# One output product per FFN over all middle values, with every transpose of those values through the DMA crossbar, in a float32 decoder trunk

## The chip, the cores and the metric

The kernel runs on one core of a Trainium2 chip. The metric is the device time of one execution in microseconds. The core has five engines that run at once and are tied together by semaphores: TensorE (PE in the profile, with PEld for its weight loads), VectorE (DVE), ScalarE (ACT), GpSimd (POOL) and SyncE (SP). SP issues plain DMAs, POOL issues DMAs that add into their target. Each engine runs its instructions in the order of the program.

## The reference

Two layers over 512 positions of width 1024, all in float32. Layer 0 mixes positions with a gated linear recurrence, layer 1 with a spatial gating unit; each mixer stands between two half-weighted feed-forward networks (FFNs) with 2816 middle values:

```python
def swiglu(x, w_in, w_out):
    g, u = jnp.split(x @ w_in, 2, axis=-1)
    return (jax.nn.silu(g) * u) @ w_out

for i in range(DEPTH):
    h = h + 0.5 * swiglu(rms_norm(h, ffn1_norm[i]), ffn1_w_in[i], ffn1_w_out[i])
    m = recurrent_mixer(...) if i % 2 == 0 else spatial_gating_mixer(...)   # on rms_norm(h, mix_norm[i])
    h = h + m
    h = h + 0.5 * swiglu(rms_norm(h, ffn2_norm[i]), ffn2_w_in[i], ffn2_w_out[i])
return rms_norm(h, final_norm)
```

So there are four FFNs. The change touches the first three: FFN 1 (before the recurrence), FFN 2 (after it) and FFN 3 (before the spatial mixer).

## The kernel before

**A product in float32.** Each float32 operand is split into a high part that TensorE's fp32r format holds and the low rest (`Sub.split`, `split`): ACT copies the high part (L97), DVE subtracts it (L88). A product is then three matmuls: high by high, low by high, high by low (L415 to L417).

**Seven products for eight.** A product of two matrices is cut into 2 x 2 blocks and made with seven block products, P1, P2, P5, P6, P3, P7, Q4, by the Winograd scheme (`seven`, L368). The left block of each is A11, A12, S1, S2, S4, S3, A22 (`LEFT`), where S1 = A21 - A22, S2 = S1 - A11, S4 = S2 + A12, S3 = -S2 - A22 are made by DVE (`Group.s2`, `s4`, `s3`). The right blocks are sums of weight blocks. A tile of raw weights (128 x 1024 floats, 512 KB) is loaded by SP (L136), and other blocks are added into it, either by an accumulating DMA from POOL (L139; `plus` is one soon after the load, `then` one after the tile's split) or by DVE from a second tile. Eight raw tiles can be live (`RAW_BUFS`, `load_more`).

**Steps.** The program is one list of steps, `subs`. A step is one of the seven products over one pair of 128-wide tiles of the contracted side: two row tiles, two tiles of the pair, three matmuls, 12 in all. The loop at L1623 walks the list: at step i it splits the weights of the steps up to i + 3 (`SPLIT_AHEAD`), runs the hooks planned for this step (phases pre, mid, rest), starts loads, and then issues the matmuls. When the last pair of a product is done, its post reads the PSUM banks. PSUM banks are named in `BANK`: P1, P6, P7 accumulate on A, P2 has B, P5 and P3 share C; Q4 has A in a chunk and its own bank Q in an output product.

**An FFN.** The 22 tiles of middle values are made in parts (`FF_PARTS`): a plain pair and a chunk of four, then twice two chunks of four. A chunk (`chunk`, L798) is one set of seven products, 14 steps, for the gate and the other half together, with SiLU and the multiplication in its posts; P3's post finishes the rows of the upper half, Q4's those of the lower. A pair (`pair_plain`, L846) is made without the scheme. Each part is followed at once by its output product (`out_blocks`, L632), seven products over the part's pairs, whose posts add 16 times into x (`upd`, L650).

**Transposes.** The middle values come out with positions on the partitions; the output product needs them the other way. Each group (one chunk or pair) is turned block by block in one of two ways (`left_blocks`, L744). By PE (`Group.stage`, `turn`, L264): transposes against an identity into PSUM (L268), from where ACT copies three blocks and DVE makes S1 of the fourth. Or by the DMA crossbar (`Group.cross`, L298), which moves 16-bit halves: ACT copies the two 16-bit planes apart (`pl`), SP issues the crossbar transposes (`dt`, L314), and five and six steps later ACT merges the planes again. In each part the pair or the first chunk of a two-chunk part goes through the crossbar, the other chunk through PE.

**Norms.** The output product of the last part calls the next norm (`norm.quarter`) as each quarter of x is done: after P2, P3, P7 and Q4.

Of the kernel before, what the change touches and what calls it, by code (L numbers as in the profile page):

```python
# [12 lines left out]
ALU = mybir.AluOpType  # L13

P = 128
# [13 lines left out]


FF_PARTS = (("p", 4), (4, 4), (4, 4))

RAW_BUFS = 8
SPLIT_AHEAD = 3
# [19 lines left out]
def trunk(ctx: ExitStack, tc: tile.TileContext, a: dict, out: bass.AP):  # L54
# [32 lines left out]
    def tt(o, x, y, op):  # L87
        nc.vector.tensor_tensor(out=o, in0=x, in1=y, op=op)  # L88
# [127 lines left out]
    def hook(n, phase, fn):  # L216


        hooks.setdefault((n, phase), []).append(fn)
# [29 lines left out]
    class Group:  # L249


        def __init__(self, n):
            self.n, self.f, self.hl = n, {}, {}
# [112 lines left out]
        return left  # L366

    def seven(block, cuts, left, w, posts, order=None, own=False, apart=False, joined=None, opening=None,  # L368
              also=None):

# [9 lines left out]
        bk, raw, held = {}, {}, []  # L380
# [49 lines left out]
        for prod, ci in order:  # L430
            if opening and (prod, ci) == ("P5", 0):
                opening[2]()

            def new(k, n, plus=None, wait=2):
                b = lambda k, n: block(k, n, cuts[ci])
                return raw_of(b(k, n), [P, len(cuts[ci]), w], plus and b(*plus), wait)

            tile = then = tile_then = None
            if prod == "P1":
                r = raw[11, ci] = new(0, 0)  # L440
                if again(ci):
                    then = block(0, 1, cuts[ci])
            elif prod == "P2":
                r = new(1, 0)
            elif prod == "P5":
                if again(ci):
                    pass
                elif own:
                    raw[11, ci] = new(0, 0, (0, 1))
                    if far(ci):  # L450
                        then = block(1, 1, cuts[ci])
                else:
                    tile = raw[12, ci] = new(0, 1)
                    tile_then = block(1, 1, cuts[ci])
                r = raw[11, ci]
            elif prod == "P6" and joined:

                tile, r, then = new(0, 1, (1, 1)), new(0, 0), block(1, 0, cuts[ci])
                raw[6, ci], raw[12, ci] = r, tile
            elif prod == "P6" and far(ci):  # L460
                r, then = raw[11, ci], block(1, 0, cuts[ci])
            elif prod == "P6":
                r, tile, then = raw[11, ci], new(1, 1), block(1, 0, cuts[ci])
                raw[22, ci] = tile
            elif prod == "P3":
                r = new(1, 1) if far(ci) or joined else raw[22, ci]
            elif prod == "P7":
                r = raw[12, ci] if joined or not own else new(0, 1, (1, 1), 2 + ci if far(ci) else 2)
            else:
                r = raw[6 if joined else 11, ci]  # L470
            subs.append(Sub(r, mm_of(prod, ci), None, tile, then, tile_then))
# [157 lines left out]
                hook(n + 4, "pre", lambda: self.take(1))  # L629


    def out_blocks(w, k0, groups, scale, norm=None, order=None, own=False, soon={}, swap=False, p2_lag=0):  # L632

        n = [g for g in groups]
        cuts, bases, i, r = [], {}, 0, k0
# [82 lines left out]
        if ends:  # L718
            order = norm.ORDER
        order = seven(block, cuts, left_of(lambda: [gs[i] for i in range(len(n))]), 512,  # L720
                      dict(P1=p1, P2=p2, P5=p5, P6=p6, P3=p3, P7=p7, Q4=q4), order, own, not ends,
                      "P3" if ends else None, also=norm.gather if ends else None)
# [75 lines left out]
    def chunk(w_in, f0, nt, group, opening=None, whole=False):  # L798


        w = nt * P
        c1, c2, c3, c5, ht = {}, {}, {}, {}, {}

        def rt(t):
            return S.rt[:, t : t + 1]

        def new(d, s, name):
            d[s] = slot(name=name)[:, :w]
            return d[s]

        def p1(s, ps):
            act(new(c1, s, "c1"), ps, AF.Copy)

        def p2(s, ps):
            tt(c1[s], c1[s], ps, ALU.add)
            hook(now[0] + (9 if opening else 1), "mid", lambda: act(c1[s], c1[s], AF.Silu, scale=rt(s)))

        def p5(s, ps):
            act(new(c5, s, "c5"), ps, AF.Copy)

        def p6(s, ps):
# [87 lines left out]

    def ffn(w_in, w_out, norm):  # L910
        f0 = 0
        for i, sizes in enumerate(FF_PARTS):
            groups, p0, pair, first = [], f0, None, not subs
            for j, n in enumerate(sizes):
                if n == "p":
                    groups.append(Group(1))
                    pair = lambda g=groups[-1], f0=f0: pair_plain(w_in, f0, g, first)
                    if not first:
                        pair()
                    f0 += 2  # L920
                else:
                    groups.append(Group(n // 2))
                    chunk(w_in, f0, n, groups[-1], (opening["A11"], opening["A12"], pair) if first else None, j == 0)
# [4 lines left out]
            soon = {("Q4", 1): 3} if last and isinstance(norm, TileNorm) else {}  # L928
# [737 lines left out]
```

## Time and profile before

| | |
|---|---|
| median of 3 runs | 1596.77 us (1595.55 to 1597.46) |
| the profiled execution: time, span | 1596.2 us, 1594.5 us |
| mean granted TensorE clock | 0.998 |
| busy PE, DVE, ACT, POOL | 1584.9, 1370.3, 1099.0, 222.2 us |
| moved by DMA | 289.79 MB, 182 GB/s on average |

The span is from the first to the last instruction. Busy time is the time in which an engine has an instruction in work; matmuls overlap each other, so that of PE says that it is occupied, not at what rate. In a group's row stand line, engine, operation, target and sources, shape and count, then busy time and mean duration in nanoseconds, then the idle time of the engine before these instructions and what ended it. In a row on a stretch stands, for each engine, its busy time in it with the number of its instructions, then granted clock, the DMA engines' mean busy share and GB/s. A wait's row gives who waited for whom, in total, how often, and the longest.

### The profile page before, as it was taken

What the parts mean: (1) busy time and instruction counts of PE and PEld (TensorE: products, weight loads), DVE (VectorE), ACT (ScalarE), POOL (GpSimd) and SP (SyncE); (2) the same over time, 40 slices, a digit from 0 to 9 for tenths busy, and PEclk for the clock granted to TensorE, in tenths of its full rate; (3) what the DMA queues carried; (4) which work ended last, traced back from release to release, by engine and by line L of the source; (5) the groups of instructions that cost most, each with busy time, mean ns of one, the idle gap of its engine ahead of it and who ended that gap; (6) DMA issues with size and microseconds to landing.
All of it is one profiled execution on the core that took longest, in us unless ns stands there. A gap on an engine that the chain in (4) does not pass through costs nothing.

```text
span 1594.5 us, 20905 instructions
## 1 busy us (share of the span) xinstructions
PE 1584.9 (99%) x7293; PEld 1313.9 (82%) x7293; DVE 1370.3 (86%) x1846; ACT 1099.0 (69%) x1615; POOL 222.2 (14%) x201
## 2 busy tenths in 40 slices
PE   9999999999999999999999999999999999999998
PEld 7878888898888888888888888888888888888886
DVE  6998887888998888978988978878978989889788
ACT  7757658668777657557776575586886876675676
POOL 2111111100010211111101111111211011111120
PEclk9999999999999999999999999999999999999999
DMA  8868878843384788878838798788878567796793
GB/s 288 193 168 194 208 177 197 209 139 106 92 211 100 178 202 207 202 175 193 201 104 195 169 201 208 181 192 203 219 197 201 158 132 198 179 223 167 175 233 94
DMA packets 208296, 289.79 MB, mean 182 GB/s; under 512 B 55504, under 2 KB 81216, under 8 KB 208192
## 3 DMA queue, kind: packets, MB, share of 16 engines
q1 hardware_dynamic: 158688, 195.33, 39.9%
q0 software_dynamic: 47712, 91.30, 34.0%
q10 hardware_dynamic: 1792, 1.84, 0.4%
q8 instruction: 57, 0.93, 0.2%
q14 instruction: 47, 0.39, 0.1%
HBM read 275.84 MB, written 2.10 MB: 174 GB/s over the span
## 4 chain that ended last, share of the span: by engine, by line
PE 94%; DMA 3%; DVE 1%; issue 0%; ACT 0%; SPq 0%; POOL 0%; POOLq 0%; ACTq 0%; DVEq 0%
PE A L415 14%; PE A L416 14%; PE A L417 14%; PE C L416 8%; PE C L417 8%; PE C L415 8%; PE p L864 4%; PE B L416 4%; PE B L417 4%; PE B L415 4%; PE e L268 2%; DMA raw<-in_ffn_w_in_dram 2%; PE r L226 2%; PE r L228 2%; PE r L227 2%; PE Q L415 1%
## 5 line engine op out<-in xcount | busy, mean ns | idle before, releaser
L97 ACT ACTIVATE whi<-raw 128x1024 fp32r<-128x1024 f32 (+1 forms) x537 | 554.7, 1034 | 330.8 <-PE A L416 78.3
L88 DVE TENSOR_TENSOR wlo<-raw,whi 128x1024 fp32r<-128x1024 f32 (+1 forms) x537 | 637.2, 1189 | 167.3 <-ACT whi L97 161.6
L415 PE MATMUL A<-whi,hi 128*128 128x512 f32 x1016 | 399.6, 393 | 0.0
L416 PE MATMUL A<-whi,lo 128*128 128x512 f32 x1016 | 395.8, 390 | 0.0
L417 PE MATMUL A<-wlo,hi 128*128 128x512 f32 x1016 | 395.8, 390 | 0.0
L415 PEld LDWEIGHTS A<-whi,hi 128*128 128x128 f32 x1016 | 190.8, 188 | 41.2 <-ACT c L97 2.9
L417 PEld LDWEIGHTS A<-wlo,hi 128*128 128x128 f32 x1016 | 190.7, 188 | 40.1 <-DVE wlo L88 0.4
L416 PEld LDWEIGHTS A<-whi,lo 128*128 128x128 f32 x1016 | 190.9, 188 | 38.9 <-DVE lo L88 0.7
L416 PE MATMUL C<-whi,lo 128*128 128x512 f32 x560 | 218.7, 391 | 1.2 <-DVE lo L88 1.2
L415 PE MATMUL C<-whi,hi 128*128 128x512 f32 x560 | 218.9, 391 | 0.5 <-ACT hi L97 0.5
L417 PE MATMUL C<-wlo,hi 128*128 128x512 f32 x560 | 218.7, 391 | 0.0
L139 POOL DMA_DIRECT2D raw<-in_ffn_w_in_dram x82 | 99.1, 1216 | 709.2 <-DVE raw L88 236.8
L139 POOL DMA_DIRECT2D raw<-in_ffn_w_out_dram x72 | 83.3, 1188 | 380.1 <-DVE wlo L88 227.9
L88 DVE TENSOR_TENSOR raw<-raw,raw 128x1024 f32<-128x1024 f32 x108 | 129.5, 1199 | 1.0
L416 PEld LDWEIGHTS C<-whi,lo 128*128 128x128 f32 x560 | 105.5, 188 | 24.0 <-DVE lo L88 2.2
L97 ACT ACTIVATE hi<-a 128x512 fp32r<-128x512 f32 (+1 forms) x188 | 111.6, 599 | 19.4 <-DVE a L88 17.2
L415 PEld LDWEIGHTS C<-whi,hi 128*128 128x128 f32 x560 | 105.5, 188 | 23.0 <-ACT hi L97 1.0
L88 DVE TENSOR_TENSOR lo<-a,hi 128x512 fp32r<-128x512 f32 (+1 forms) x188 | 121.8, 654 | 2.2 <-ACT hi L97 2.1
L417 PEld LDWEIGHTS C<-wlo,hi 128*128 128x128 f32 x560 | 105.4, 188 | 21.8
L416 PE MATMUL B<-whi,lo 128*128 128x512 f32 x280 | 109.0, 389 | 0.1
L415 PE MATMUL B<-whi,hi 128*128 128x512 f32 x280 | 109.0, 389 | 0.0
L417 PE MATMUL B<-wlo,hi 128*128 128x512 f32 x280 | 108.9, 389 | 0.0
(184 smaller groups left out, 2096.8 us busy)
## 6 DMA issues: line engine op xcount, KB each, us to landing
raw<-in_ffn_w_in_dram SPq DMA_DIRECT2D x161, 512.0 KB, 4.6
raw<-in_ffn_w_out_dram SPq DMA_DIRECT2D x100, 512.0 KB, 5.6
raw<-in_ffn_w_in_dram POOLq DMA_DIRECT2D x82, 512.0 KB, 7.1
raw<-in_ffn_w_out_dram POOLq DMA_DIRECT2D x60, 512.0 KB, 7.8
raw<-in_sg_w_in_dram SPq DMA_DIRECT2D x20, 512.0 KB, 6.9
raw<-in_ffn_w_in_dram SPq DMA_DIRECT2D x34, 256.0 KB, 4.8
raw<-in_rec_w_in_dram SPq DMA_DIRECT2D x16, 512.0 KB, 3.9
raw<-in_sg_w_in_dram POOLq DMA_DIRECT2D x12, 512.0 KB, 7.4
```

What stands on the lines that cost most here:

```text
L88: nc.vector.tensor_tensor(out=o, in0=x, in1=y, op=op)
L97: nc.scalar.activation(out=o, in_=x, func=f, **k)
L139: nc.gpsimd.dma_start(out=self.v, in_=src, accum_op=ALU.add)
L226: nc.tensor.matmul(ps, wh, xh, start=start, stop=False)
L227: nc.tensor.matmul(ps, wh, xl, start=False, stop=False)
L228: nc.tensor.matmul(ps, wl, xh, start=False, stop=stop)
L268: nc.tensor.transpose(ps[:, o : o + P], src(q, s), ident)
L415: nc.tensor.matmul(ps, zh, wh, start=fresh and i == 0, stop=False, **k)
L416: nc.tensor.matmul(ps, zl, wh, start=False, stop=False, **k)
L417: nc.tensor.matmul(ps, zh, wl, start=False, stop=end, **k)
L864: nc.tensor.matmul(bank_of(half, s), z, (sub.lo if m == 2 else sub.hi)[:, q, :], start=left[2] == "2" and (h, q, m) == (0, 0, 0), stop=lef ...
```

## The change

In the first three FFNs all middle values are made first: the pair and five chunks, one after the other. One output product over all six groups (11 pairs of tiles, in six sets: one for the pair, five of two pairs) follows. The last FFN, whose norm ends the kernel, stays as it was.

- `FF_WHOLE` is the one part; `Group.whole` is set on all its groups. Their blocks go through the crossbar, without the splits and sums that `left_blocks` planned.
- `out_blocks` plans these by step instead: for each step of the output product the split of its left block, three steps ahead (four for P7 and Q4 before the tile norm), and ahead of P6, P3 and P7 the sum S2, S4 or S3.
- The order of the 42 steps is `CHAIN`: P1 over six sets, P2 over six, then P5, P6 and four of Q4 interleaved, then P3 and P7 interleaved and the last two of Q4.
- The weight tiles are chained. P5's tile (one load, one accumulation) goes on to P6 (a second tile added by DVE) and, after one more accumulation, to Q4, as before. P3 now loads a tile of its own and after an accumulation that tile serves P7; before, P3 used P6's second tile, and P7 loaded one and accumulated.
- In the first FFN the opening of the kernel stays with the pair and the first chunk.

```diff
+FF_WHOLE = (("p", 4, 4, 4, 4, 4),)
+CHAIN = ([("P1", i) for i in range(6)] + [("P2", i) for i in range(6)]
+         + [("P5", 0), ("P5", 1), ("P6", 0), ("P5", 2), ("P6", 1), ("P5", 3), ("P6", 2), ("Q4", 0), ("Q4", 1),
+            ("P5", 4), ("P6", 3), ("Q4", 2), ("P5", 5), ("P6", 4), ("Q4", 3), ("P6", 5)]
+         + [("P3", 0), ("P3", 1), ("P3", 2), ("P3", 3), ("P7", 0), ("P7", 1), ("P3", 4), ("P7", 2), ("P3", 5),
+            ("P7", 3), ("P7", 4), ("P7", 5), ("Q4", 4), ("Q4", 5)])
...
             tile = then = tile_then = None
-            if prod == "P1":
+            if chain:
+                if prod in ("P1", "P2"):
+                    r = new(int(prod == "P2"), 0)
+                elif prod == "P5":
+                    r = raw[11, ci] = new(0, 0, (0, 1))
+                elif prod == "P6":
+                    r, tile, then = raw[11, ci], new(1, 1), block(1, 0, cuts[ci])
+                elif prod == "P3":
+                    r, then = new(1, 1), block(0, 1, cuts[ci])
+                    raw[33, ci] = r
+                else:
+                    r = raw[33 if prod == "P7" else 11, ci]
+            elif prod == "P1":
...
+        sums_of = dict(P6=lambda ci: gs[ci].s2(), P3=lambda ci: gs[ci].s4(), P7=lambda ci: gs[ci].s3()) if chain else {}
         for i, (prod, ci) in enumerate(order):
-            if prod in ("P3", "P6", "P7", "Q4"):
+            if chain or prod in ("P3", "P6", "P7", "Q4"):
                 lead = 6 if ends and prod == "P3" else 4 if (ends or isinstance(norm, TileNorm)) and prod in ("P7", "Q4") else 3 if 1 in n else 2
                 lead = soon.get((prod, ci), lead)
+                if prod in sums_of:
+                    hook(at0 + i - lead, "pre", lambda ci=ci, fn=sums_of[prod]: fn(ci))
                 hook(at0 + i - lead, "mid", lambda ci=ci, name=LEFT[prod]: gs[ci].parts(name))
...
         n = now[0] + lag
+        if g.whole:
+            hs = [tiles[2 * half + s] for s in range(2)]
+            if half:
+                for h in hs:
+                    tt(h[:, : g.n * P], h[:, : g.n * P], h[:, g.n * P :], ALU.subtract)
+            g.cross(half, hs, (n, "mid"), ((n + 5, "mid"), (n + 6, "mid")), ())
+            return
...
-        for i, sizes in enumerate(FF_PARTS):
+        chain = not hasattr(norm, "last")
+        all_parts = FF_WHOLE if chain else FF_PARTS
+        for i, sizes in enumerate(all_parts):
...
-            last, mixed = i == len(FF_PARTS) - 1, "p" in sizes
+            last, mixed = i == len(all_parts) - 1, "p" in sizes and not chain
...
-            gs = out_blocks(w_out, p0, [g.n for g in groups], 0.5, norm if last else None, own=True, soon=soon,
-                            swap=mixed, p2_lag=6 * mixed)
+            gs = out_blocks(w_out, p0, [g.n for g in groups], 0.5, norm if last else None, CHAIN if chain else None,
+                            own=True, soon=soon, swap=mixed, p2_lag=6 * mixed, chain=chain)
```

More of the change, by code (lines that the diff above doesn't have):

```diff
@@ L252, in __init__ @@
         def __init__(self, n):
-            self.n, self.f, self.hl = n, {}, {}
+            self.n, self.f, self.hl, self.whole = n, {}, {}, False
         def new(self, name):
@@ L368, in seven @@
     def seven(block, cuts, left, w, posts, order=None, own=False, apart=False, joined=None, opening=None,
-              also=None):
+              also=None, chain=False):
         bk, raw, held = {}, {}, []
@@ L629, in quarter, with out_blocks @@
                 hook(n + 4, "pre", lambda: self.take(1))
-    def out_blocks(w, k0, groups, scale, norm=None, order=None, own=False, soon={}, swap=False, p2_lag=0):
+    def out_blocks(w, k0, groups, scale, norm=None, order=None, own=False, soon={}, swap=False, p2_lag=0, chain=False):
         n = [g for g in groups]
@@ L721, in out_blocks @@
                       dict(P1=p1, P2=p2, P5=p5, P6=p6, P3=p3, P7=p7, Q4=q4), order, own, not ends,
-                      "P3" if ends else None, also=norm.gather if ends else None)
+                      "P3" if ends else None, also=norm.gather if ends else None, chain=chain)
+        sums_of = dict(P6=lambda ci: gs[ci].s2(), P3=lambda ci: gs[ci].s4(), P7=lambda ci: gs[ci].s3()) if chain else {}
         for i, (prod, ci) in enumerate(order):
-            if prod in ("P3", "P6", "P7", "Q4"):
+            if chain or prod in ("P3", "P6", "P7", "Q4"):
                 lead = 6 if ends and prod == "P3" else 4 if (ends or isinstance(norm, TileNorm)) and prod in ("P7", "Q4") else 3 if 1 in n else 2
                 lead = soon.get((prod, ci), lead)
+                if prod in sums_of:
+                    hook(at0 + i - lead, "pre", lambda ci=ci, fn=sums_of[prod]: fn(ci))
                 hook(at0 + i - lead, "mid", lambda ci=ci, name=LEFT[prod]: gs[ci].parts(name))
@@ L916, in ffn @@
                     groups.append(Group(1))
+                    groups[-1].whole = chain
                     pair = lambda g=groups[-1], f0=f0: pair_plain(w_in, f0, g, first)
@@ L922, in ffn @@
                     groups.append(Group(n // 2))
-                    chunk(w_in, f0, n, groups[-1], (opening["A11"], opening["A12"], pair) if first else None, j == 0)
+                    groups[-1].whole = chain
+                    chunk(w_in, f0, n, groups[-1],
+                          (opening["A11"], opening["A12"], pair) if first and j == 1 else None, j == 0)
                     f0 += n
-            last, mixed = i == len(FF_PARTS) - 1, "p" in sizes
+            last, mixed = i == len(all_parts) - 1, "p" in sizes and not chain
             if mixed:
                 groups.reverse()
-            soon = {("Q4", 1): 3} if last and isinstance(norm, TileNorm) else {}
-            gs = out_blocks(w_out, p0, [g.n for g in groups], 0.5, norm if last else None, own=True, soon=soon,
-                            swap=mixed, p2_lag=6 * mixed)
+            soon = {("Q4", len(groups) - 1): 3} if last and isinstance(norm, TileNorm) else {}
+            gs = out_blocks(w_out, p0, [g.n for g in groups], 0.5, norm if last else None, CHAIN if chain else None,
+                            own=True, soon=soon, swap=mixed, p2_lag=6 * mixed, chain=chain)
             gs.update(enumerate(groups))
```

## The prediction

> **What bounds the kernel now.** I read the page first: the busy shares, the granted clock, the chain that ended last and the two big DMA queues.
>
> ```profile
> span 1594.5 us, 20905 instructions
> PE 1584.9 (99%) x7293; PEld 1313.9 (82%) x7293; DVE 1370.3 (86%) x1846; ACT 1099.0 (69%) x1615; POOL 222.2 (14%) x201
> ...
> PE 94%; DMA 3%; DVE 1%; issue 0%; ACT 0%; SPq 0%; POOL 0%; POOLq 0%; ACTq 0%; DVEq 0%
> ...
> q1 hardware_dynamic: 158688, 195.33, 39.9%
> q0 software_dynamic: 47712, 91.30, 34.0%
> ```
>
> TensorE (PE) is the bound, in the chain as in the busy time. A busy PE can still be a slow one, so next I read busy time in stretches: a first chunk of an FFN part, the second chunk with the first steps of the output product, the rest of that output product, and the same middle stretch one part later.
>
> ```profile
> core 0: us, PE busy (x) PEld busy (x) DVE busy (x) ACT busy (x) POOL busy (x), PEclk, DMA share, GB/s
> ...
> 571.98:610.06 38.08, 38.08 (x168) 31.27 (x167) 30.98 (x33) 22.78 (x29) 4.82 (x4) 1.00 0.75 182
> 610.06:652.78 42.72, 42.72 (x198) 35.54 (x197) 35.70 (x41) 33.40 (x44) 7.68 (x7) 1.00 0.92 220
> 652.78:688.24 35.46, 35.46 (x160) 29.37 (x158) 34.10 (x43) 18.30 (x24) 4.39 (x4) 1.00 0.70 166
> 730.00:771.00 41.00, 41.00 (x191) 34.13 (x190) 34.16 (x39) 31.08 (x41) 9.63 (x8) 1.00 0.98 225
> ```
>
> The first stretch is one chunk: 14 steps of 12 matmuls, 168 in 38.08 us, so 0.227 us a matmul and 2.72 us a step. The others keep that rate at clock 1.00, although DVE stands at 96% in the third and the DMA engines at 98% in the last. So PE does not wait there, and only two things can shorten the run: PE instructions that disappear, and the few places where PE is slower than 0.227 us. The weight loads' waits name those places; the last rows show the worst.
>
> ```profile
> PEld A L415 <- ACT c L97: 2.9, 8, 0.4
> PEld C L416 <- DVE lo L88: 2.2, 5, 1.5
> PEld C L415 <- ACT hi L97: 1.0, 1, 1.0
> ...
> 80.56 0.19 PEld L415 LDWEIGHTS C<-whi,hi 128*128 128x128 f32 x1 [0.97 <-ACT hi L97]
> 82.24 0.19 PEld L416 LDWEIGHTS C<-whi,lo 128*128 128x128 f32 x1 [1.49 <-DVE lo L88]
> ...
> 79.60:88.00 8.40, 6.68 (x21) 4.79 (x20) 8.40 (x17) 5.00 (x8) 2.09 (x2) 0.80 0.41 85
> ```
>
> **The change, part by part.** Matmuls of the products: each of the first three FFNs has three output products over 6, 8 and 8 tiles of middle values now and one over 22 after, so the same 42 steps and the same loads of weights: per group and seven products, five plain loads and three accumulating ones, before and after (P3 loads its own tile and P7 accumulates on it, where P3 used P6's tile and P7 loaded). I price that at zero.
>
> *Transposes off PE.* Three groups of four tiles per FFN go through PE now, 16 blocks each: 3 x 3 x 16 = 144 of the 224 blocks in the row below, in 18 batches of 8. Each batch takes 0.87 us of the chain (a first and a last one of the FFNs in question):
>
> ```profile
> 172.63 0.87 PE e L268 x8
> ...
> 1094.77 0.87 PE e L268 x8
> ...
> L268 PE MATMUL e<-ident,c 128*128 128x128 f32 x224 | 29.3, 272 | 0.0
> L97 ACT ACTIVATE a<-dt 128x1024 uint16<-128x1024 uint16 (+1 forms) x36 | 36.3, 1009 | 0.0
> L97 ACT ACTIVATE pl<-c 128x512 uint16<-128x512 uint16 x64 | 36.0, 622 | 7.7 <-DVE c L94 6.0 <-DVE c L88 1.7
> L97 ACT ACTIVATE a<-e 128x512 f32<-128x512 f32 x42 | 24.5, 584 | 0.6 <-PE e L268 0.6
> L94 DVE SCALAR_TENSOR_TENSOR x<-A,x 128x512 f32<-128x512 f32 x112 | 71.4, 680 | 6.4 <-PE A L417 6.3
> ```
>
> 18 x 0.87 = 15.7 us, all of it on the path, since PE waits for nothing around them. Bounds: 15.7 by the chain, 144/224 x 29.3 = 18.8 by the overlapping busy times. I take 15.7, which is a difference of starts.
>
> *What the crossbar adds.* Nine groups take the other path: each 8 plane copies and 4 merges on ACT in place of 3 copies, 8 x 0.622 + 4 x 1.009 - 3 x 0.584 = 7.3 us, 65 us in all, so ACT goes from 1099 to about 1164 us (73%). In a chunk ACT has 22.78 of 38.08 us now; with all 9.0 us of a whole group it is under 32. That is hidden behind PE; without that cover it would be 65 us. The SP queue issues 72 more transposes:
>
> ```profile
> L314 SPq DMA_TRANSPOSE dt<-pl x96: 1183/1216/2134, 44.9 to 1516.2; - x96
> who waited for it (us, times):
> DMA to landing us min/median/max: 2.3/3.0/9.2
> ```
>
> So four hold SP for 4.9 us, and the weight loads behind them wait that long and for the plane copies. By the program's order a load stands six or more steps (16 us) ahead of its split, so it is late by nothing. Nothing waits long for these transposes now; in the last chunk the merged blocks are due five steps later (13.6 us) and need 4 x 0.622 + 4 x 1.216 + 3.0 + 1.0 = 11.4 us.
>
> One cost is visible. A crossed chunk puts its plane copies in front of P7's copy on ACT, and Q4's first matmul waits for that copy (it accumulates on the same bank):
>
> ```profile
> 252.72 0.39 PE L416 MATMUL A<-whi,lo 128*128 128x512 f32 x1
> 252.94 0.39 PE L417 MATMUL A<-wlo,hi 128*128 128x512 f32 x1
> 253.27 0.50 PE L415 MATMUL A<-whi,hi 128*128 128x512 f32 x1
> 253.61 0.40 PE L416 MATMUL A<-whi,lo 128*128 128x512 f32 x1
> ```
>
> 0.33 + 0.34 instead of 0.45 is 0.21 us, in each of the eight crossed chunks (the row of eight waits above). Nine more give +1.9 us. Bounds: 0 (a later copy order) and 9 x 1.0 = 9 us, if a fuller ACT is late by a whole split; I take 1.9, the row of the same work.
>
> *Fewer additions into x.* 16 a part, two parts fewer in three FFNs: 96 x 0.680 = 65 us of DVE, down to about 1305 us. DVE bounds nothing now except at the one place below, so by itself this is worth 0. What DVE gains is room in the output product, where it stands at 96%.
>
> *The stall at 80 us.* It lies in the first FFN's first output product: 21 matmuls in 8.40 us, 21 x 0.227 = 4.8, so 3.6 us lost. Behind it stand a split that waited for an accumulating load and a DVE without a gap:
>
> ```profile
> 75.40 1.06 ACT L97 ACTIVATE whi<-raw 128x1024 fp32r<-128x1024 f32 x1 [2.73 <-DMA raw<-in_ffn_w_out_dram]
> ```
>
> After the change that product does not follow there; a chunk does, whose first steps split plain loads and need no splits of blocks. Bounds 0 to -3.6, or up to +3.6 if the eight more transposes in the busy opening delay loads there; I take -3.6, because the load, the accumulation and the additions that made it are gone from the place. The loss is part idle and part clock: the granted clock is 0.80 over that stretch. The Trainium skill, "TensorE: Matmul & The Clock Gate" (section "Why this matters for your kernels"), sets gaps of some 3 us as what lowers the clock. This trace differs: gaps of 0.97 and 1.49 us were enough, and the measurement decides.
>
> *The chained tiles.* By the order of the program and eight buffers, the stretch of 18 steps (49 us) around the interleaved P5/P6/Q4 asks for 9 accumulating and 12 plain loads of 512 KB. From the queue rows an accumulating one costs 34.0% x 1594.5 / 91.30 x 0.524 = 3.1 us of all DMA engines, a plain one 39.9% x 1594.5 / 195.33 x 0.524 = 1.7 us: 28 + 20.5 = 48.5 us, 99%. Now the highest stretch is 98% over 41 us, without a wait on PE. An accumulation has four steps to land (three for the last P7), and splits run three steps ahead of PE: 10.9 + 8.2 less two passes of 1.0 and 1.2 us leaves 14.7 us, against
>
> ```profile
> raw<-in_ffn_w_out_dram POOLq DMA_DIRECT2D x60, 512.0 KB, 7.8
> ```
>
> so I price it at 0, with 0 to +13 us per FFN as bounds (the upper end is worked out below). POOL issues in order, so a late accumulation holds the next; they are 1 to 2 steps apart.
>
> **Sum.** 1594.5 - 15.7 - 3.6 + 1.9 = 1577.1 us of span. The profiled execution took 1596.2 us, 1.7 over its span, and the median of the runs is 1596.8: 17.4 less gives 1579.4.
>
> **The rivals.** (1) *Part of the gain is eaten on ACT and in the opening.* Nine chunks at up to 1.0 us and a stall at 80 us that stays: 1596.8 - 15.7 + 9 = 1590. For it: ACT's load rises by 6%, all in the chunks. Against: the eight crossed chunks lose only 0.21 us.
>
> (2) *The accumulating queue becomes the bound* (the slower side). At 99% any extra price counts. If accumulations cost 5.5 us each when both queues compete, 9 x 5.5 + 20.5 = 70 us in 49, less 8.2 of lead, leaves 12.8 us per FFN, and each such gap lowers the clock as at 80 us, where 3.6 less the two gaps of 2.5 leaves 1.1: 3 x 13.9 - 17.4 = +24, 1621. It turns the sign from about (17.4/3 + 8.2 + 49 - 1.1 - 20.5)/9 = 4.6 us each. Against: at 98% the engines still moved 225 GB/s and PE waited for nothing.
>
> (3) *The crossbar's latency stands on the path* at the start of each output product: 11.4 us exposed once per FFN, 3 x 11.4 - 17.4 = +17, 1614. Against: the empty list of waiters above, and 13.6 us of room.
> Here the Trainium skill, "VectorE: DVE Perf Modes" (section "Rules for kernel authors"), speaks against the change: transpose 128x128 on TensorE where PSUM will do, through the crossbar otherwise; its table has 390 ns on TensorE and 1309 ns on the crossbar. By that rule the transposes should have stayed. The trace agrees that the crossbar is the slower path (1216 ns of issue alone against 0.87 us for eight blocks), but not that it is the dearer one here, where PE is full and SP is not.
>
> (4) *It does little*: new waits of about 17 us in all give back the gain, 1594 to 1600.
>
> **How the numbers follow.** Forecast 0.62 (1576 to 1583), rival 1 0.18 (1583 to 1593.6), rival 4 0.05, rival 2 0.10, rival 3 0.05. The first two hold 0.80, so the range is 1576 to 1594. Its low end is the sum without the 1.9 us (1577.5) with 1.5 off for the higher transpose price. 0.2% is 3.2 us, about what these runs tell from no change (they span 1595.55 to 1597.46). Faster 0.80, same 0.05, slower 0.15.
>
> **What would show it.** In the changed kernel's groups: 80 blocks e<-ident,c instead of 224, 168 crossbar transposes instead of 96, 96 fewer additions into x. In the waits: 17 waits of weight loads on ACT's c copy instead of eight, no gap near 80 us, clock 1.00 throughout. DVE near 1305 us, ACT near 1164, PE near 1569. I am wrong if PE waits on splits inside the output product (steps P5 to P7), with the splits waiting for accumulating loads; or if plane copies or merges wait for SP; or if a buffer of the slot pool comes free late, which no row here shows.

## The result and the profile after

The changed kernel takes **1605.22 us** (median of 4, 1603.93 to 1606.85) against 1596.16 before on the same chip (1595.41 to 1597.46): ratio **1.0056, 95% interval 1.0039 to 1.0074**. It is slower, where 1579.4 was forecast. First the page: span, TensorE, DVE and ACT, the two big DMA queues, and the chain that ended last.

```profile
span 1605.0 us, 20741 instructions
PE 1581.6 (99%) x7149; PEld 1304.4 (81%) x7149; DVE 1315.6 (82%) x1759; ACT 1158.9 (72%) x1696; POOL 222.5 (14%) x201
...
q1 hardware_dynamic: 197856, 204.78, 41.4%
q0 software_dynamic: 47712, 91.30, 33.9%
...
PE 79%; DMA 6%; issue 5%; DVE 4%; ACT 2%; POOL 1%; ACTq 0%; SPq 0%; POOLq 0%
```

PE has 144 matmuls less and DVE 55 us less, as meant; the accumulating queue (q0) moves the same bytes in nearly the same share. But the chain was PE for 94% and is PE for 79% now: DMA, "issue" and DVE have come into it. The weight loads' longest waits, and ACT's splits that waited for a weight tile, after and then before:

```profile
PEld A L421 <- ACT c L103: 7.9, 17, 2.3
PEld e L274 <- DVE x L100: 7.8, 4, 4.5
PEld C L422 <- DVE lo L94: 4.1, 8, 0.9
PEld xt L615 <- ACT xn L103: 3.6, 1, 3.6
```
```profile
ACT whi L103 <- DMA raw<-in_ffn_w_out_dram: 35.5, 16, 4.5
```
```profile
ACT whi L97 <- DMA raw<-in_ffn_w_out_dram: 3.0, 2, 2.7
```

Splits of w_out's tiles waited 3.0 us for a load before, 35.5 us now. PE feels it last, at the end of an output product: `e<-ident,x` and `xt<-ident,xn` are transposes of the next norm, which need the last post of P3 or P7.

To put places to the loss I took, for each PE instruction, the distance from its start to the next one's start less the median distance of its kind, and added these up by stretch. All the kernels run below are in the table; the last column but one holds mostly the edges of crossed chunks.

```
us lost by PE       0-50  50-75 75-100  product: FFN1  FFN2  FFN3   rest   all
before               1.2    0.2    3.9           0.7   0.4   0.4    3.0    9.7
after                1.9    2.3    0.0          12.4   7.7   7.0    4.2   35.5
e1_no_acc            1.7    3.8    0.0           1.3   0.1   0.3    4.5   11.6
e8_half_acc          0.9    3.9    0.0           1.4   0.1   0.3    4.3   10.6
e2_no_sums           1.5    3.9    0.0           7.3   1.2   3.2    4.4   21.4
e12_sums_early       1.4    3.8    0.0          11.2   3.5   4.6    4.4   28.8
e4_tail              1.6    2.3    0.0          12.1   2.9   3.8    4.5   27.1
e3_pe_turn           1.9    0.2    0.0          10.4   2.9   2.9    3.6   21.8
e9_last_pe           1.3    3.8    0.0           9.2   5.2   8.0    4.1   31.5
e5_planes            1.6    0.1    0.0          12.2   5.2   6.3    1.5   26.8
e13_order_only       1.5    1.9    0.0           9.7   5.2   1.8    4.6   24.7
e6_order             1.7    2.3    0.0           8.2   2.7   1.7    4.3   20.8
e7_both              1.8    0.1    0.0          11.3   2.5   1.0    1.3   17.8
e10_early            1.8    0.1    0.0           4.3   3.6   2.1    1.2   13.2
e11_gates            1.7    0.1    0.0           2.9   2.4   2.6    1.4   10.9
e14_spread           1.4    0.1    0.0           2.0   3.2   2.1    1.4   10.2
```

The account closes: 1594.5 before, 35.5 - 9.7 = 25.8 more lost, 1605.0 after; so the transposes took 15.3 us with them, and the three output products lose 27.1 us where the stretches lost 1.5. Some 17 of the 27.1 lie in the last seven of a product's 42 steps. The second FFN's product in stretches of 12 us:

```profile
core 0: us, PE busy (x) PEld busy (x) DVE busy (x) ACT busy (x) POOL busy (x), PEclk, DMA share, GB/s
...
712.00:724.00 12.00, 12.00 (x55) 9.93 (x54) 10.96 (x15) 10.34 (x14) 3.31 (x3) 1.00 0.99 260
724.00:736.00 12.00, 12.00 (x59) 10.04 (x58) 9.61 (x15) 7.03 (x13) 3.34 (x3) 1.00 1.06 286
736.00:748.00 12.00, 12.00 (x54) 9.93 (x53) 8.52 (x12) 7.72 (x15) 3.65 (x3) 1.00 1.07 221
748.00:760.00 12.00, 11.79 (x52) 9.23 (x50) 11.92 (x14) 7.73 (x11) 1.20 (x1) 1.00 0.81 190
760.00:772.00 12.00, 12.00 (x54) 9.95 (x53) 12.00 (x17) 7.39 (x10) 3.53 (x4) 1.00 0.97 260
772.00:784.00 12.00, 12.00 (x54) 9.95 (x53) 11.85 (x18) 7.27 (x10) 3.54 (x4) 1.00 1.03 184
784.00:796.00 12.00, 12.00 (x54) 9.95 (x53) 10.11 (x14) 5.41 (x8) 2.26 (x2) 1.00 1.04 256
796.00:808.00 12.00, 7.75 (x28) 5.96 (x27) 7.40 (x10) 9.13 (x17) 0.00 (x0) 0.72 0.50 159
```

The DMA engines are full from 712 to 748, and nearly so again from 760 to 796. In the third row DVE is idle for 3.5 of 12 us: it waits for splits that wait for tiles. From 748 it has no room (11.92, 12.00, 11.85 of 12), and what it was late it stays. PE shows almost nothing until its lead is used up; then the last accumulation falls due. ACT's three long waits for a tile, then the chain of waits through the end of the product (start, duration, what):

```profile
726.47 1.06 ACT L103 ACTIVATE whi<-raw 128x1024 fp32r<-128x1024 f32 x1 [2.65 <-DMA raw<-in_ffn_w_out_dram]
...
746.98 1.06 ACT L103 ACTIVATE whi<-raw 128x1024 fp32r<-128x1024 f32 x1 [3.06 <-DMA raw<-in_ffn_w_out_dram]
...
796.97 1.06 ACT L103 ACTIVATE whi<-raw 128x1024 fp32r<-128x1024 f32 x1 [4.54 <-DMA raw<-in_ffn_w_out_dram]
```
```profile
788.53 8.34 DMA raw<-in_ffn_w_out_dram
...
796.97 1.06 ACT whi L103
...
798.06 0.56 DVE wlo L94
...
799.20 0.68 DVE lo L94
799.89 0.22 DVE x L100
...
801.14 1.75 PE e L274 x7
```

That is P7's last tile. Its accumulation is issued when P3's last split is done, three steps (8.2 us) before its own split is due, and lands after 8.34 us. Behind the late split, in order on DVE, stands P3's addition into x, and behind that the norm's transposes: PE stands for 4.1 us, and the clock of that stretch falls to 0.72. A part of the loss is this slow clock: after such gaps the granted clock was 0.50 for 20.4 us in the three products, two of the four stretches in the first FFN's:

```profile
331.20:338.00 6.80, 5.94 (x22) 5.46 (x23) 6.34 (x13) 6.32 (x13) 0.00 (x0) 0.50 0.59 170
798.80:805.60 6.80, 4.93 (x15) 4.05 (x16) 6.54 (x9) 6.09 (x13) 0.00 (x0) 0.50 0.54 160
```

The other two are 276.6 to 280.0 and 1129.9 to 1133.3 us. At half the clock that is some 10 of the 27.1 us (an estimate, half of 20.4): 5.1, 3.4 and 1.7 in the three products.

The gap at 80 us is gone, and one at 64 us has come. ACT's queue there, and PE:

```profile
63.19 0.63 ACT L103 ACTIVATE pl<-c 128x512 uint16<-128x512 uint16 x1
64.58 1.67 ACT L103 ACTIVATE pl<-c 128x512 uint16<-128x512 uint16 x3 [0.76 <-DVE c L100]
66.15 1.06 ACT L103 ACTIVATE c<-A 128x512 f32<-128x512 f32 x2
```
```profile
66.78 0.50 PE L421 MATMUL A<-whi,hi 128*128 128x512 f32 x1 [1.88 <-ACT c L103]
```

Plane copies of the opening's chunk wait for DVE's c; P7's copy out of bank A is queued behind them, and Q4's first matmul waits for it, 1.88 us.

### The profile page after: what moved, and what is told of

Same layout as the page of the kernel before. It is cut to its first block, busy times and chain, and to the rows that moved or that the text cites. A ratio compares the mean times of both kernels' runs of the same rounds, so it can differ in the third digit from the quotient of the medians.

```text
span 1605.0 us, 20741 instructions
## 1 busy us (share of the span) xinstructions
PE 1581.6 (99%) x7149; PEld 1304.4 (81%) x7149; DVE 1315.6 (82%) x1759; ACT 1158.9 (72%) x1696; POOL 222.5 (14%) x201
## 3 DMA queue, kind: packets, MB, share of 16 engines
q0 software_dynamic: 47712, 91.30, 33.9%
## 4 chain that ended last, share of the span: by engine, by line
PE 79%; DMA 6%; issue 5%; DVE 4%; ACT 2%; POOL 1%; ACTq 0%; SPq 0%; POOLq 0%
PE A L421 12%; PE A L422 12%; PE A L423 12%; PE C L422 6%; PE C L423 6%; PE C L421 6%; DMA raw<-in_ffn_w_out_dram 6%; PE p L892 4%; PE B L421 3%; PE B L423 3%; PE B L422 3%; PE r L232 2%; PE r L234 2%; PE r L233 2%; PE e L274 1%
## 5 line engine op out<-in xcount | busy, mean ns | idle before, releaser
L94 DVE TENSOR_TENSOR raw<-raw,raw 128x1024 f32<-128x1024 f32 (+1 forms) x108 | 129.6, 1200 | 0.9
L422 PEld LDWEIGHTS C<-whi,lo 128*128 128x128 f32 x560 | 105.1, 188 | 25.8 <-DVE lo L94 4.1
```

Of the source, the lines that this page charges most:

```text
L422: nc.tensor.matmul(ps, zl, wh, start=False, stop=False, **k)
```

## The experiments

The kernel before ran beside each group of runs (medians 1595.4 to 1596.8). "Lost in the products" is the sum of the table's three columns: 27.1 after, 1.5 before.

**1. No accumulating loads in the chained product.**

```diff
-                    r = raw[11, ci] = new(0, 0, (0, 1))
+                    r = raw[11, ci] = new(0, 0)
...
-                    r, tile, then = raw[11, ci], new(1, 1), block(1, 0, cuts[ci])
+                    r, tile = raw[11, ci], new(1, 1)
...
-                    r, then = new(1, 1), block(0, 1, cuts[ci])
+                    r = new(1, 1)
```

> The changed kernel, with the accumulating DMAs of the chained output product left out (18 per FFN; the right blocks of P5 to Q4 then lack one summand each, so part of the computation is missing). Plain loads, splits, sums and their order stay. Theory A, the accumulating transfers come due faster than the DMA engines serve them, ACT and DVE wait for them and lose their lead over PE: PE's lost time in the three output products (about 27 us) goes, 1578 to 1582. Theory B, DVE has more work between P5 and P7 than PE gives it time, and the waits for DMA only happen to lie there: most of the loss stays, 1597 or more.

Measured 1581.22 us, ratio 0.9906 (0.9890 to 0.9923); lost in the products 1.7. So everything else in the change is worth what the forecast said to 2 us (1581.2 against 1579.4; against the kernel beside it, 14.7 us gained of 17.4), and the accumulations' presence costs 24.0 us, nearly the whole of the miss of 25.8. No split waits for a tile of w_out any more. The crossbar, the plane copies and a full DVE are all still there:

```profile
748.00:760.00 12.00, 12.00 (x55) 9.93 (x54) 11.34 (x17) 7.04 (x10) 0.00 (x0) 1.00 0.28 93
784.00:796.00 12.00, 12.00 (x63) 10.11 (x62) 10.25 (x14) 10.41 (x22) 0.00 (x0) 1.00 0.57 173
```

**2. Accumulations of half the size**, as many, in the same order and queue: P5's, Q4's and P7's bring `src[:, :1]` of their tiles (those of the pair's set are 256 KB anyway and stay as they were).

```diff
-            nc.gpsimd.dma_start(out=self.v, in_=src, accum_op=ALU.add)
+            nc.gpsimd.dma_start(out=self.v[:, : src.shape[1]], in_=src, accum_op=ALU.add)
```

> The changed kernel where each accumulating load of the chained output product brings only the first half of its tile (256 KB in place of 512 KB; the sum in the other half is left out, so the product is not the reference's). Same number of accumulations, same order, same queue. Theory A, by rate: an accumulation then asks for 1.55 us of the DMA engines, less than a plain load, the 6-step peak falls from 1.24 to about 0.98 and the lead is not used up: 1581 to 1588. Theory L, by latency and order (an accumulating load must follow a split and land before the next, whatever its size): most of the loss stays, 1597 to 1605.

Measured 1581.56, ratio 0.9913 (0.9898 to 0.9928), lost in the products 1.7: as if there were none. Not their number or their turn behind the splits cost the time, but their bytes: the load that these put on the DMA engines, or the time that they take to land, which fell with it. The run does not separate the two. Its DMA issues (size, median from issue to landing), of which 45 of the 57 are the halved ones and the 15 those of the fourth FFN:

```profile
raw<-in_ffn_w_out_dram POOLq DMA_DIRECT2D x57, 256.0 KB, 4.6
raw<-in_ffn_w_out_dram POOLq DMA_DIRECT2D x15, 512.0 KB, 8.1
```

The size alone does not set that time. In the changed kernel itself the pair's accumulations take as long as those of twice their size:

```profile
raw<-in_ffn_w_out_dram POOLq DMA_DIRECT2D x60, 512.0 KB, 7.5
...
raw<-in_ffn_w_out_dram POOLq DMA_DIRECT2D x12, 256.0 KB, 7.4
```

**3. No block sums.** S2, S4 and S3 of the chained groups are left out (`if not self.whole:` ahead of the three operations in `s2`, `s4`, `s3`).

> The changed kernel, with the 18 sums S2, S4, S3 per chained output product left out (the left blocks of P6, P3, P7 are then wrong): 11.5 us less of DVE work per FFN, all between P5 and P7; DMA as it was. Theory A: the waits of the splits for accumulating loads stay (2.7 and 3.1 us early in each product), the lead is won back sooner, 1588 to 1600. Theory B: the loss goes, 1582 or less.

Measured 1593.75, ratio 0.9987 (0.9978 to 0.9997); lost in the products 11.7. **4. The sums early**: formed as soon as their operands are there, in the first 25 steps of the product.

```diff
-                    hook(at0 + i - lead, "pre", lambda ci=ci, fn=sums_of[prod]: fn(ci))
+                    n2 = max(order.index((p, ci)) for p in (("P1",) if ci < 5 else ("P5",))) - 1
+                    n2 = max(n2, order.index(("P1", ci)) - lead + 1, 2 * (ci == 4))
+                    at = {"P6": n2, "P3": max(n2, order.index(("P2", ci)) - lead) + 1,
+                          "P7": max(n2, order.index(("P5", ci)) - lead) + 2}[prod]
+                    at = min(at, i - lead)
+                    hook(at0 + at, "pre", lambda ci=ci, fn=sums_of[prod]: fn(ci))
```

> The changed kernel, its order and its plane copies untouched, with the block sums formed as soon as their operands are there. Leaving the sums out gave 1593.8, 11.4 us less. Theory V (it is where the sums stand that costs: they follow the late splits in a stretch in which DVE has no room to catch up): half to all of that comes back, 1593 to 1600. Rival (DVE's total in the product is what counts, or the late loads alone): 1603 to 1607.

Measured 1598.55, ratio 1.0010 (0.9999 to 1.0021), lost in the products 19.3. With less work on DVE in the tight part, late tiles cost PE less, and more than half of what leaving the sums out brought is had by moving them. ACT's waits for w_out's tiles in the two runs, sums left out and sums early:

```profile
ACT whi L103 <- DMA raw<-in_ffn_w_out_dram: 66.4, 31, 6.7
```
```profile
ACT whi L103 <- DMA raw<-in_ffn_w_out_dram: 53.8, 22, 5.3
```

They wait longer than the 35.5 us of the changed kernel and run faster. So a wait on a tile is no cost in itself; it costs where the engines behind it cannot win it back. That these runs wait longer because DVE is back at the front sooner is how I read it; no run shows it.

**5. The last link two steps longer**: P3's last two ahead of P7's second, so that the last accumulation has five steps, not three.

```diff
-[...] ("P7", 0), ("P7", 1), ("P3", 4), ("P7", 2), ("P3", 5),
+[...] ("P7", 0), ("P3", 4), ("P3", 5), ("P7", 1), ("P7", 2),
```

> The changed kernel, with the end of the step order changed: P3 of the last two sets comes before P7 of the second set, so that an accumulating load between P3 and P7 has five steps where the last had three. Theory D, the last link of the chain is too short by itself and holds the norm at the end of each product (3.2, 4.1 and 2.2 us): 1594 to 1597. Theory A, the link is only late because the lead was lost before: it helps in part, 1597 to 1603. Theory B: no change, 1603 to 1607.

Measured 1598.89, ratio 1.0018 (1.0009 to 1.0028): 6.3 us less, all of it in the second and third FFN (14.7 to 6.7 lost). The first FFN's loss (12.1, of 12.4) is not that link's.

**6. The chain alone**, transposes on PE or crossbar as before (`if g.whole and whole:` ahead of the crossing, and chunks 2 and 4 crossed).

> The chained output product alone: transposes on the same paths as in the kernel before (pair, second and fourth chunk through the crossbar, first, third and fifth chunk through PE). Theories A and B, the loss lies in the output product and the crossbar is innocent: 18 batches of 0.87 us come back and nine waits of 0.21 us go, 1605 + 15.7 - 1.9 = 1619 (1614 to 1624). Theory C, the 72 further crossbar transposes (SP queue, 7.3 us of ACT per group) delay the loads: at or below the changed kernel, 1590 to 1606.

Measured 1609.42, ratio 1.0087 (1.0058 to 1.0116), between the theories. It puts 15.7 us of transposes back and costs 4.2 in the medians, with executions from 1604.67 to 1616.29: lost in the products 16.2, no gap at 64 us. **7. Only the last chunk on PE**, the one beside the product (`j < 5 if chain else j == 0` in the call of `chunk`, and the same condition).

> The changed kernel with only the last chunk of each FFN back on TensorE for its transposes, 6 batches of 8 at 0.87 us = 5.2 us more on the path; the other chunks stay on the crossbar. If the crossbar beside the output product is what cost the 7 us that the run with all transposes on their old paths left unexplained: 1605.2 + 5.2 - 7 = 1603.4 (1601 to 1606). If it is not beside the product: 1609 to 1612. The gap near 64 us stays in both.

Measured 1606.68, ratio 1.0076 (1.0053 to 1.0099), in no band: 5.2 us put back for 1.5, lost in the products 22.4. So the crossbar's path near the product deepens the loss by some 5 to 11 us in these profiles; but it does so only with the accumulations, since run 1 has all of it and loses 1.7. Whether that is its copies and merges on ACT, its issues on SP or its share of the DMA engines, the two runs do not show.

**8. Plane copies two steps later** (one in the kernel's opening) in the first four of an FFN's five chunks, behind P7's copy. The expectation speaks of five, but `j` counts the pair as 0, so the edit reaches four; its 12 edges are those of four chunks in three FFNs.

```diff
-                left_blocks(group, ht, 0, 2 if opening else 1, whole=whole)
+                left_blocks(group, ht, 0, group.lag or (2 if opening else 1), whole=whole)
...
+                    groups[-1].lag = 3 * (chain and j < 5)
```

> The changed kernel, with the plane copies of the first five chunks of each FFN one step later on ACT, behind P7's copy into the bank; the last chunk's stay. Theory E (two of the lost terms are only the order on ACT): the gap near 64 us (2.3 us of TensorE time) and the crossed edges of these chunks (about 12 x 0.21 = 2.5 us) go: 1605.2 - 4.8 = 1600.4, with the waits of weight loads on ACT's c copy down from 17 to some 5. Rival (these waits only move to the merges, which now come later in front of the output product and beside the DVE's sums): no gain, 1604 to 1607.

Measured 1598.10, ratio 1.0018 (1.0007 to 1.0030), 7.1 less. The gap at 64 us is gone (0.1), the rest falls from 4.2 to 1.5; both were an order on ACT. The rest came out of the products (27.1 to 23.7).

**9. Another order and P1's tile for P5.** P1 and P2 are interleaved, P5 and P6 spread between them, and P5 accumulates onto P1's tile, so that a group asks for four plain and three accumulating loads. (The kernel before shares that tile only in its very last product; in the first three FFNs it asks for five and three, as the changed kernel does.) **10. The order alone**, P5 with its own load.

```diff
+CHAIN = [(p[:2], int(p[2])) for p in (
+    "P10 P11 P12 P20 P13 P21 P14 P22 P15 P50 P23 P51"
+    " P60 P24 P52 P61 P25 P53 P62 Q40 P54 P63 Q41 P55 P64 Q42 P65 P30 Q43 P31 P32 P33 P34 P70 P35 P71 P72 P73 P74 P75 Q44 Q45").split()]
...
+                if prod == "P1":
+                    r, then = new(0, 0), block(0, 1, cuts[ci])
+                    raw[11, ci] = r
...
                 elif prod == "P5":
-                    r = raw[11, ci] = new(0, 0, (0, 1))
+                    r = raw[11, ci]
```

> The changed kernel with another order of its 42 steps: P2 and P1 interleaved, P5 between them, Q4 four steps later, P3 before P7; and P5 accumulates onto P1's tile, as the kernel before does, so that a group asks for four plain and three accumulating loads in place of five and three. By the same price list (3.1 us an accumulating load, 1.7 a plain one) its highest stretches ask for 1.06 of the DMA time over 6 steps, 0.98 over 12 and 0.90 over 18, where the changed kernel asks for 1.24, 1.13 and 0.99; an accumulation has five steps or more. Theory A (short peaks of DMA demand that run the lead down): most of the 27 us lost in the three output products come back: 1605.2 - 27 + 0 to 6 = 1578 to 1584. Theory C (the crossbar beside the output product): at most a few us, 1598 to 1604. The opening gap and the crossed edges stay in both.

> The other order of steps alone: P5 loads its own tile again, as in the changed kernel, so a group asks for five plain and three accumulating loads (18 more plain loads of 512 KB over the three FFNs than the run with order and shared tile). By the same price list its highest stretches ask for 1.18 of the DMA time over 6 steps, 1.06 over 12 and 1.03 over 18 (changed kernel 1.24, 1.13, 0.99; with the shared tile 1.06, 0.98, 0.90), while an accumulation still has five steps or more. Theory R (the demand in the peaks is what counts): most of the 13 us that order and shared tile gained together are the tile's, 1598 to 1604. Theory O (the order counts: room for each accumulation, P3 ended before P7): 1590 to 1594.

Measured 1592.27, ratio 0.9980 (0.9970 to 0.9989), with both, which is faster than before by 0.2% but 8 us over the band; 1596.28, ratio 1.0004 (0.9994 to 1.0014), with the order alone, between its two theories. Of 13 us the order brings 9 and the shared tile 4. What both leave is mostly in the first FFN (8.2 and 9.7), where ACT's `xn` holds the norm. The waits of weight loads in run 9:

```profile
PEld A L419 <- ACT c L101: 8.0, 17, 2.3
PEld xt L616 <- ACT xn L101: 4.0, 1, 4.0
```

**11. Order, tile and later plane copies together**, the copies now in all five chunks (the expectation speaks of six, but the sixth group is the pair, whose copies stay).

> The other order of steps (with P5 accumulating onto P1's tile) and the later plane copies together, these now in all six chunks of an FFN. If the two losses are separate, their gains add: 1592.3 - (1605.2 - 1598.1) = 1585 (1583 to 1588), with no gap near 64 us and no weight load that waits for ACT's c copy. Rival (the plane copies and merges of the last chunk, two steps later, now fall into the first steps of the output product and hold its blocks): 1589 to 1594.

Measured 1589.42, ratio 0.9947 (0.9932 to 0.9962): the rival's band. On top of run 9 the planes bring 2.9, not 7.1; gap and edges go, but the first FFN's product loses 3 more. **12. With the sums early** as in run 4; **13. with the recurrent gates' loads 14 steps earlier** (`at0 - 48`, not `at0 - 34`); **14. with S3's sums six steps ahead of their use**, not up to seventeen.

> As the run with order and planes together, and DVE's block sums S2, S4 and S3 of the chained groups are formed as soon as their operands are there (2 to 17 steps earlier, in the first 25 of the 42 steps) and no longer three steps ahead of their use. Theory V (in the second half of the product DVE is full, 12 of 12 us in the stretches that lose time, while in the first half it is busy 8.5 to 11 of 12): the sums, 16 x 0.65 = some 11 us an FFN, move into room, and the gap of 3.6 us at the end of the first FFN and the smaller ones of the others shrink: 1578 to 1583. Rival (DVE's sums are not what is late; the norm's own reads are): 1584 to 1587, as without.

> As the run with early sums, and the loads of the recurrent gates' weights (four small transfers of many pieces during the first FFN's output product) start 14 steps earlier, ahead of that product. If these transfers add to what the first FFN loses: 1 to 3 us less than with early sums alone. If not: within 1 us of it.

> The run with early gate loads, where DVE then was full (12 of 12 us) from the tenth step of the second FFN's output product to the twenty-sixth and had room behind: there C's weight loads wait for DVE's lo, 5.7 us in all, and TensorE loses about 7 us in the three products. Here the five S3 sums of an FFN are formed six steps ahead of their use, not up to seventeen, so that they fall behind that stretch. If DVE's load in the middle is what is left: 1577 to 1581. If the waits are for other reasons: 1581 to 1584.

Run 12: 1585.55 (ratio 0.9926, 0.9912 to 0.9941), 3.9 less than run 11 but in the rival's band. The gap of the first FFN's end, of which the theory spoke, is gone (11.3 to 4.3 lost); the other two products lose 2.2 us more, now in their first half, where the sums went. Run 13: 1582.22 (0.9906, 0.9891 to 0.9921), 3.3 less, so the gates' small transfers may add to the loss; but the two intervals just overlap, and the table finds only 1.4 us of it in the first FFN, the one with the gates, and 1.2 in the second. Run 14: **1581.03 (0.9904, 0.9889 to 0.9919)**, on the edge of its two bands; 1.2 us below run 13 are well inside both intervals. From its product of the second FFN, the stretch of its worst loss and the two at the end (columns as above):

```profile
700.00:712.00 12.00, 11.02 (x46) 8.27 (x45) 7.46 (x11) 7.50 (x10) 1.20 (x1) 1.00 0.86 196
...
772.00:784.00 12.00, 12.00 (x59) 10.01 (x58) 10.29 (x14) 10.73 (x20) 0.00 (x0) 1.00 0.90 260
784.00:796.00 12.00, 12.00 (x59) 10.03 (x58) 9.80 (x13) 7.44 (x13) 0.00 (x0) 1.00 0.60 169
```

It beats both kernels, by 15 us and 24 us, with all sums and three accumulations a group in place, one plain load a group fewer and the gates' loads moved: most of the loss lay in where the chained loads, the copies and the sums stood.

## Why the prediction was wrong

**The step that failed** is "The chained tiles", priced "at 0, with 0 to +13 us per FFN as bounds". Its term measured 24.0 us over three FFNs (after less run 1), 8 a product: inside the bounds, which the range did not take in, since its upper end stopped at rival 1. It is also where the prediction's own sign of being wrong showed: PE waited on splits from P5 to P7, and the splits for accumulating loads. Three things in its working were wrong.

- *The average.* By the prediction's own prices (3.1 and 1.7 us), 99% over 18 steps holds 6 steps at 1.24 and 12 at 1.13 of what the engines can move, as counted for run 9. A short peak cost nothing before: the DMA share is 1.05 from 734.2 to 766.9 us there, and PE does not wait. What is new is how long it lasts. The highest stretch of 84 us before, and the one of the second FFN's product after:

```profile
1061.80:1145.80 84.00, 84.00 (x396) 70.06 (x395) 75.00 (x99) 62.15 (x97) 15.84 (x14) 1.00 0.94 229
```
```profile
712.00:796.00 84.00, 83.79 (x373) 68.98 (x372) 74.97 (x100) 52.88 (x76) 20.83 (x18) 1.00 1.00 237
```

  DVE has as much to do in both rows; the DMA engines do not. Before, a chunk came after the peak, and there DVE had 30.98 of 38.08 us to do; after the change the product goes on, with DVE at 11.92, 12.00 and 11.85 of 12 us in the next three stretches. Run 10, at 1.03 over 18 steps, is 9 us faster than the changed kernel at 0.99: such a mean does not even order the kernels.
- *The lead.* The three steps by which splits run ahead were counted as 8.2 us of slack for each accumulation, as if the lead were whole each time. It is one stock, used up by the tiles at 726 and 747 us and not refilled; at 797 us a landing of 8.34 us against three steps of 8.2 met no lead (run 5: 6.3 us).
- *The cover.* "DVE bounds nothing now" priced the removed additions at 0, and took the room in DVE's mean for room in the product. Runs 3 and 4 show that DVE's room there decides how much of the lateness becomes lost PE time: 27.1 us fell to 11.7 without the sums and to 19.3 with the sums early.

**Rival 2** named the place (accumulations, output product), not the cause: the price of an accumulation did not rise, 33.9% x 1605.0 / 91.30 x 0.524 = 3.1 us as before. Inside the second FFN's product, from 712 to 796 us, it was the same, 60.7% x 84 / 8.65 x 0.524 = 3.1 us:

```profile
q0 software_dynamic: 4509, 8.65, 60.7%
```

So its turning point of 4.6 us was never reached. No dearer queue was needed, only no room to recover.

**The other terms.**
- *Transposes off PE*, -15.7: 15.3 by the account above. 80 blocks and 168 crossbar transposes, as forecast:

```profile
L274 PE MATMUL e<-ident,c 128*128 128x128 f32 x80 | 10.5, 272 | 0.0
...
L320 SPq DMA_TRANSPOSE dt<-pl x168: 1180/1210/3023, 45.4 to 1526.5; - x168
```

- *The stall at 80 us*, -3.6: -3.9 there, and +2.1 at 64 us (0.2 to 2.3; 3.8 or 3.9 in five of the runs below), so the opening gained 1.8 us or next to nothing. The bound "up to +3.6 if the eight more transposes in the busy opening delay loads there" was right that the opening pays for the transposes, but the cause was not a load: it was the order on ACT, which run 8 mends.
- *The crossed edges*, +1.9: 17 waits came, as forecast, and the rest of the table rose by 1.2; 2.7 went with run 8.
- *DVE near 1305*: 1315.6. The 96 additions took 61.7 us with them in the rows' busy time, where 96 x 0.680 = 65 counts each as if none overlapped the next. A crossed group subtracts on DVE twice, once for each of two row tiles, where a turned one subtracts once: 9 more instructions, so 87 fewer in all. The rest of the difference is not accounted for. ACT near 1164: 1158.9. PE near 1569 and a clock of 1.00 throughout did not come: 1581.6 us, and 0.992 on average in the profiled execution.
- *Rival 3*, the crossbar's latency: in run 1, with 168 crossbar transposes and no accumulation, the products lose 1.7 us, so by itself it costs nothing. Beside late tiles the crossbar's path does (runs 6 and 7). The Trainium skill, "VectorE: DVE Perf Modes" (section "Rules for kernel authors"), would have kept the transposes on TensorE; run 6, which puts them back, takes 1609.42 us against 1605.22, so here the rule gains nothing, even where the crossbar's path does harm.

*What stays open*: why the first FFN's product loses most (12.4 us, of which the slow clock is some 5; run 5 took nothing off it, run 7 some 3, and early sums only in the new order, in run 12); and how the 24 us divide between the DMA and DVE, since less load on the DMA engines removes the whole loss and less work on DVE a little more than half of it.

## What to carry to other kernels

Price a chain of transfers by its due times, not by a mean share of the DMA engines: go along the steps, keep the lead as one stock, and ask where the consumer has room to win it back. If a cost has bounds that could turn the sign and nothing in the trace decides between them, the range must hold them. And the cure need not be to undo: another order of steps, copies, sums and small loads placed where there is room, and one tile used twice made a change that lost 9 us gain 15.

## What the runs showed of the hardware

The same gap at 64 us, 1.88 us in the changed kernel and 1.85 us in run 1, lowered the granted clock in one execution and not in the other. The stretches behind it, after and run 1:

```profile
68.00:72.00 4.00, 4.00 (x19) 3.25 (x19) 3.66 (x5) 3.04 (x5) 0.00 (x0) 1.00 1.32 216
```
```profile
68.00:72.00 4.00, 4.00 (x12) 3.06 (x12) 2.62 (x4) 1.82 (x3) 0.00 (x0) 0.60 1.07 198
```

19 matmuls in 4 us at 1.00, 12 at 0.60. Over the nine kernels with this gap the table has 3.8 or 3.9 us in five and 1.9 to 2.3 in four: a gap just under 2 us costs about itself or twice itself, so a term for such a gap needs both ends. The Trainium skill, "TensorE: Matmul & The Clock Gate" (section "Why this matters for your kernels"), puts the gaps that lower the clock at some 3 us; here one of 1.85 us did. And the time from issue to landing of an accumulating load did not go by its bytes alone: 256 KB took 4.6 us at the median in run 2, where the DMA engines had less to move, and 7.4 us in the changed kernel, where 512 KB took 7.5.
